# Second layer of a hybrid diffusion block: latent tiles 1 and 2 take one pass together through queries, output projection and routing

## The chip, the cores and the metric

The kernel runs on one core of a Trainium2 chip, one launch per call. The metric is the device time of that launch in microseconds. All data are float32 in HBM; the large matrix products of the second half of each layer split each operand into two rounded parts on chip.

## The reference, cut to what matters

512 latent tokens `x` and 256 context tokens `ctx`, each 1024 wide, pass two layers:

```python
for l in range(2):
    a = modulate(h, norm1)                      # adaLN shift and scale
    p = a @ w_in[l]                             # queries, compressed keys/values
    q_m = rms(rms(qa) @ wuq)  ; q_s = rms(sq)   # two head groups, 8 heads each
    o = concat(latent_attention(q_m, k, v), window_attention(q_s, k, v))
    h = h + g1 * (o @ w_out[l])
    b = modulate(h, norm2)
    # PEER: product-key retrieval, per token and each of 8 heads
    s   = (b @ wq) . sub_keys                   # 2 x 128 scores per head
    top16 of each half -> 256 sums -> top16 -> idx, g = softmax
    a   = gelu(b . u[idx])                      # 128 rows of u per token
    h   = h + g2 * sum((g * a) * v[idx])        # 128 rows of v per token
```

`u` and `v` have 16384 rows of 1024 for each layer. In the second layer the context tokens only give keys and values; their queries, projection and experts are left out.

## The kernel before, in words

Tokens are handled in tiles of 128: latent tiles 0 to 3, context tiles 0 and 1. For each layer the program lists generators, each of which emits the instructions of one step for one or more tiles: `KV` (keys and values), `Q` (queries: loads of `w_in` and `wuq`, `project_q`), `A` (`attend`, two times four pairs of heads), `O` (`out_proj`: eight loads of `w_out`, gated residual, second norm, the transposed input `bT`), `R` (`route`: sixteen loads of `wq`, matrix products, products with the sub-keys, and for each of 16 halves `max`, `max_index`, `match_replace`, `max`, `max_index` on DVE), `G` and `GH` (`choose`, the top 16 of the sums, again on DVE; `GH` then calls `one_hots`). `RF` is `R` for one tile with half of its `choose` inside. `run` emits generators one after the other; `par` mixes them by their lengths. `Q`, `O` and `R` take a tuple of tiles: then each weight is loaded once and used for all of them (L434 and L459, L572, L639 to L644).

The expert stage of layer 2 has two ways. Tiles 2 and 3 (`DENSE[1]`) go the dense way: `one_hots` writes a table of gates to HBM (`Gd`), and `dense_experts` then loads all of `u` and `v` in 128 iterations, splits them on ACT and DVE (L867, L868), multiplies on PE (L921, L894) and weights by the gates on DVE (L927). Tiles 0 and 1 go by lookups (`experts`): one lookup is one indirect gather of 512 KB, issued by POOL (L754) into one of five buffers `gv`, and one pass on DVE (L758 for a row of `u`, L768 for a row of `v`). A tile takes 128 lookups in `u` and 128 in `v`, so tiles 0 and 1 have 512 in all, in that order. 40 lookups left from the first layer run at the start of layer 2 (`left`).

`AHEAD[1]` is 0.72: 368 of the 512 lookups are emitted ahead of the dense loop, the other 144 are laid by hand into its iterations from the 16th on (`LATE`, `manual_schedule`). Everything else is ordered for each engine by a scheduler that simulates the program while it is built: the written order is only a priority. So lookups stand on DVE in between the instructions of attention, routing and choosing, and each engine runs its list strictly in order. All weight loads go through SP's queue and share four buffers `w4` of 512 KB, which sets how far loads run ahead.

```python
for _ in range(int(n * AHEAD[l])):
    next(rows)
es.enter_context(tc.manual_schedule(engines=MANUAL))
```

Of the kernel before, what the change touches and what calls it, by code (L numbers as in the profile page):

```python
# [89 lines left out]
def body(ctx: ExitStack, tc: tile.TileContext, I, out):  # L90
# [191 lines left out]
    def layer_consts(l):  # L282
        k = {}
        n = 2 * QK + 2 * SD + H
        g = cst.tile([P, n], F32, tag="gains", name="gains")
        src = I["gains"]
        nc.sync.dma_start(g, bass.AP(tensor=src.tensor, offset=src.offset + l * n, ap=[[0, P], [1, n]]))
        k["nsink"] = g[:, 2 * QK + 2 * SD:]
        nc.vector.tensor_scalar(k["nsink"], k["nsink"], -1.0, None, op0=OP.mult)
        k["g_mq"], k["g_mk"] = g[:, NOPE:QK], g[:, QK + NOPE:2 * QK]  # L290
        k["g_sq"], k["g_sk"] = g[:, 2 * QK:2 * QK + SD], g[:, 2 * QK + SD:2 * QK + 2 * SD]
        cols = cst.tile([P, 9], F32, tag="gcols", name="gcols")
        nc.sync.dma_start(cols, I["gcols"][l])
        k["qa_g"], k["kva_g"] = cols[:, 0:3], cols[:, 3:5]

        nc.vector.tensor_scalar(cols[:, 5:6], cols[:, 5:6], QK ** -0.5, None, op0=OP.mult)
        nc.vector.tensor_scalar(cols[:, 7:8], cols[:, 7:8], SD ** -0.5, None, op0=OP.mult)
        k["mq_ctx"], k["mk_ctx"], k["sq_ctx"], k["sk_ctx"] = (cols[:, i:i + 1] for i in range(5, 9))
        lat = cst.tile([P, 2], F32, tag="glat", name="glat")
        nc.vector.memset(lat[:, 0:1], QK ** -0.5)  # L300
        nc.vector.memset(lat[:, 1:2], 1.0)
        nc.vector.tensor_copy(lat[:NOPE, :], cols[:NOPE, 5:7])
        k["mq_lat"], k["mk_lat"] = lat[:, 0:1], lat[:, 1:2]
        return k
# [357 lines left out]
    def chosen(dn):  # L662
        return [exp.tile([P, P], F32, tag=x + dn, name=x, bufs=2) for x in ("ef", "g")]
# [283 lines left out]
    def norms(l, st, tiles, m, keep):  # L947

        aT = []
        for i in tiles:  # L950
            t = fm_tile("aT")
            aT.append(t)
            if (l, st, i) in kept:
                nc.sync.dma_start(t, kept.pop((l, st, i)))
                continue
            modulated_T(t, h_load(st, i), m[1], m[0], J[st])
            if keep:
                kept[l, st, i] = tc.dram_tile([P, KC, P], F32, name=f"aT_{st}{i}")
                nc.sync.dma_start(kept[l, st, i], t)
        return aT  # L960
# [18 lines left out]
    def run(*gens):  # L979
        for g in gens:  # L980
            for _ in g:
                pass

    def par(*gens):

        live = [[0, n, g] for g, n in gens]
        while live:
            x = min(live, key=lambda x: x[0] / x[1])
            x[0] += 1
            if next(x[2], x) is x:  # L990
                live.remove(x)

    mods = [[] for _ in range(L)]
    for l in range(L):
        m = mods[l]
        js, ds, got = [], [], {}
        Gd = tc.dram_tile([P, len(DENSE[l]) * P // GT, NK, GT], F32, name="Gd")
        with ExitStack() as es:
            pool = lambda nm, bufs, **k: es.enter_context(tc.tile_pool(name=f"{nm}{l}", bufs=bufs, **k))
            att, tmp, rou, sm = pool("att", 1), pool("tmp", 2), pool("rou", 1), pool("sm", 2)  # L1000
            psb = pool("psb", 2, space=bass.MemoryType.PSUM)
            psm = pool("psm", 1, space=bass.MemoryType.PSUM)
            K = layer_consts(l)
            kv = {"kT": att.tile([QK, H, C + S], F32, tag="kT", name="kT"),
                  "v": att.tile([P, (C + S) // P, H * VD], F32, tag="v", name="v"),
                  "skT": att.tile([P, 2, C + S], F32, tag="skT", name="skT"),
                  "sv": att.tile([P, (C + S) // P, 2 * SD], F32, tag="sv", name="sv")}
            qs, os, bs = {}, {}, {}

            def KV(st, *tiles):  # L1010
                aT = norms(l, st, tiles, m, st == "lat")
                yield
                yield from project_kv(l, st, tiles, aT, K, kv)

            def Q(st, *tiles):
                aT = norms(l, st, tiles, m, False)
                yield
                yield from project_q(l, st, tiles, aT, K, qs)

            def KVQ(st, *tiles):  # L1020
                aT = norms(l, st, tiles, m, False)
                yield
                yield from project_kv(l, st, tiles, aT, K, kv)
                yield from project_q(l, st, tiles, aT, K, qs)

            def A(st, i):
                os[st, i] = yield from attend(l, st, i, *qs.pop((st, i)), K, kv)

            def O(*tiles):
                res = yield from out_proj(l, tiles, [os.pop(x) for x in tiles], m)  # L1030
                bs.update(zip(tiles, res))

            def R(*tiles):
                b = [bs.pop(x) for x in tiles]
                res = yield from route(l, [x[0] for x in b])
                for x, r, y in zip(tiles, res, b):
                    got[x] = r, y[1], None

            def RF(st, i):

                bT, bd = bs.pop((st, i))
                half = chosen("")

                def mid(res):
                    yield from choose(*res[0], *half, 0, H // 2)

                r, = yield from route(l, [bT], mid)
                got[st, i] = r, bd, half

            def G(st, i):  # L1050
                yield from go(l, st, i, m, got, js, ds)

            def GH(i, wide=False):
                yield from go(l, "lat", i, m, got, js, ds)
                yield from one_hots(ds, len(ds) - 1, Gd, wide)

            c, t = "ctx", "lat"
            if l == 0:
                a = ada(l, m)
                next(a)  # L1060
                run(KVQ(c, 0, 1))
                run(a, A(c, 0), O((c, 0)))
                early = qs[c, 1][1][:, 0, 0:1]
                par((A(c, 1), 16), (R((c, 0)), 16))
                run(G(c, 0), ada(1, mods[1], early))
                run(KV(t, 0, 1), KV(t, 2, 3), Q(t, 0, 1), A(t, 0), O((c, 1), (t, 0)))
                par((A(t, 1), 8), (R((c, 1), (t, 0)), 24))
                run(G(c, 1), O((t, 1)), Q(t, 2, 3))
                par((A(t, 2), 8), (R((t, 1)), 24), (GH(0), 48))
                run(O((t, 2)))  # L1070
                par((A(t, 3), 8), (R((t, 2)), 24), (GH(1), 48))
                run(O((t, 3)))
                par((R((t, 3)), 24), (GH(2, True), 48))
                run(G(t, 3))
            else:
                run(KV(c, 0, 1), KV(t, 0, 1), Q(t, 0), left, KV(t, 2, 3), A(t, 0), O((t, 0)))
                run(RF(t, 0), Q(t, 1), A(t, 1))
                run(G(t, 0), O((t, 1)), Q(t, 2, 3))
                par((A(t, 2), 8), (R((t, 1)), 24))
                run(G(t, 1), O((t, 2)))  # L1080
                par((A(t, 3), 8), (R((t, 2)), 24))
                run(O((t, 3)))
                par((R((t, 3)), 24), (GH(2), 48))
                run(GH(3, True))
        with ExitStack() as es:
            den = es.enter_context(tc.tile_pool(name=f"den{l}", bufs=1))
            psd = es.enter_context(tc.tile_pool(name=f"psd{l}", bufs=1, space=bass.MemoryType.PSUM))
            rows = experts(js)
            n = 256 * len(js)
            dense = dense_experts(l, ds, Gd, m, den, psd)  # L1090
            next(dense)
# [3 lines that stand above are left out]
            free[0] = False  # L1095
            rest = n - int(n * AHEAD[l]) - SPILL[l]
            for e, _ in enumerate(dense):
                for _ in range(rest * max(0, e + 1 - LATE[l]) // (NK - LATE[l]) - rest * max(0, e - LATE[l]) // (NK - LATE[l])):
                    next(rows, None)
            if not SPILL[l]:  # L1100
                run(rows)
            left = rows
            free[0] = True
# [56 lines left out]
```

## Time and profile before

| what | value |
|---|---|
| median of 3 runs | 4489.13 us (4487.55 to 4492.19) |
| the profiled execution | 4481.78 us, its span 4480.0 us |
| busy, share of the span | PE 81%, PE's weight loads 65%, DVE 75%, ACT 38%, POOL 36% |
| DMA | 1306.48 MB, mean 292 GB/s |
| 640 gathers of `u`, 640 of `v` | 784.6 and 782.1 us of POOL's time |

Layer 2 begins at about 2530 us. Tile 0's lookups begin at 2867 us, when half of its experts are chosen; the dense loop's first iteration ends its first product at 3646 us; the program ends at 4480 us. All times in the text are microseconds from the span's start. An engine that is busy for most of a stretch is not yet the bound: what ended the waits in that stretch must be read beside it.

### The profile page before, as it was taken

How to read it: one execution, taken by the hardware profiler on the slowest of the kernel's cores; microseconds unless marked ns; L12 is line 12 of the kernel's file. 1: busy time of each engine (PE TensorE's matmuls, PEld its weight loads, DVE VectorE, ACT ScalarE, POOL GpSimd, SP SyncE). 2: the span in 40 equal slices, each digit the busy share in tenths (PEclk: the TensorE clock that was granted, in tenths of full speed). 3: DMA queues.
4: the chain of work that ended last, by engine and by line, in shares of the span. 5: the costliest groups of instructions: out<-in, count | busy, mean ns of one | idle time of the engine just before them, and what ended most of it. 6: DMA issues, size and time to landing. Idle time of an engine off the chain costs nothing.

```text
span 4480.0 us, 58044 instructions
## 1 busy us (share of the span) xinstructions
PE 3617.1 (81%) x19934; PEld 2907.9 (65%) x19934; DVE 3352.5 (75%) x7566; ACT 1687.4 (38%) x3244; POOL 1629.0 (36%) x1402
## 2 busy tenths in 40 slices
PE   6885778477887999999999668676676468999997
PEld 2453357256776898888988545444455467888886
DVE  1247778989678788777877832778989977777777
ACT  1342231155575333333333234232224653444443
POOL 2016565544101444444444510255443443222222
PEclk8997788788997999999999889898888579999999
DMA  8588898888666999999999952789899789889897
GB/s 303 171 284 305 307 346 310 299 300 311 219 204 229 327 318 315 325 334 328 332 311 318 330 175 92 258 320 336 310 335 345 260 307 337 301 298 304 298 316 245
DMA packets 467481, 1306.48 MB, mean 292 GB/s; under 512 B 41568, under 2 KB 147808, under 8 KB 467184
## 3 DMA queue, kind: packets, MB, share of 16 engines
q0 software_dynamic: 199744, 726.26, 46.0%
q1 hardware_dynamic: 267440, 576.50, 37.0%
q8 instruction: 157, 2.57, 0.2%
q14 instruction: 140, 1.15, 0.1%
HBM read 1240.70 MB, written 61.90 MB: 291 GB/s over the span
## 4 chain that ended last, share of the span: by engine, by line
PE 24%; issue 24%; DVE 23%; DMA 13%; ACT 8%; POOL 7%; SPq 0%; POOLq 0%; ACTq 0%; DVEq 0%
DVE vacc L768 8%; POOL gv L754 7%; PE m L644 5%; DVE v L868 4%; ACT u L867 3%; DMA gv<-v,idx 3%; DVE gv L758 2%; DMA gv<-u,idx 2%; PE m L372 2%; DMA raw<-uT 2%; PE acc L852 2%; PE A L921 2%; DMA w<-w_in 2%; PE o L894 2%; PE m L507 1%
## 5 line engine op out<-in xcount | busy, mean ns | idle before, releaser
L754 POOL DMA_INDIRECT gv<-v,idx x640 | 782.1, 1222 | 1143.4 <-DVE vacc L768 807.3
L754 POOL DMA_INDIRECT gv<-u,idx x640 | 784.6, 1226 | 964.3 <-DVE a L758 635.4
L894 PE MATMUL o<-v,W 128*128 128x512 f32 x3840 | 943.0, 398 | 71.3 <-ACT W L867 71.0
L921 PE MATMUL A<-b,u 128*128 128x384 f32 (+1 forms) x6144 | 962.5, 313 | 41.6 <-ACT w L924 29.8
L921 PEld LDWEIGHTS A<-b,u 128*128 128x128 f32 x6144 | 936.3, 192 | 70.8 <-ACT w L924 39.3
L894 PEld LDWEIGHTS o<-v,W 128*128 128x128 f32 x3840 | 719.0, 191 | 228.9 <-ACT W L867 84.6
L768 DVE SCALAR_TENSOR_TENSOR vacc<-gv,a,vacc 128x1024 f32<-128x1024 f32 x635 | 811.2, 1277 | 55.7 <-DMA gv<-v,idx 48.5
L758 DVE CUSTOM_DVE_ANT_0 gv<-gv,btok 128x1024 f32<-128x1024 f32 x640 | 768.0, 1218 | 98.0 <-DMA gv<-u,idx 97.1
L867 ACT ACTIVATE W<-w 128x384 fp32r<-128x384 f32 (+1 forms) x256 | 120.7, 472 | 1042.5 <-DVE w L927 1042.5
L868 DVE TENSOR_TENSOR u<-raw,u 128x1024 fp32r<-128x1024 f32 x256 | 313.5, 1224 | 166.3 <-ACT u L867 164.1
L372 PE MATMUL m<-w,aT 128*128 128x256 f32 (+3 forms) x704 | 259.7, 518 | 86.7 <-DMA w<-w_in 51.4
L644 PE MATMUL m<-bT,wq 128*128 128x128 f32 x2560 | 313.7, 279 | 5.0 <-DMA wq<-wq 4.1
L868 DVE TENSOR_TENSOR v<-raw,v 128x1024 fp32r<-128x1024 f32 x256 | 311.9, 1218 | 3.6 <-ACT v L867 3.5
L644 PEld LDWEIGHTS m<-bT,wq 128*128 128x128 f32 x2560 | 301.1, 195 | 10.7 <-DMA wq<-wq 5.7
L867 ACT ACTIVATE u<-raw 128x1024 fp32r<-128x1024 f32 x256 | 267.7, 1046 | 62.5 <-DMA raw<-uT 62.5
L867 ACT ACTIVATE v<-raw 128x1024 fp32r<-128x1024 f32 x256 | 267.4, 1044 | 4.6 <-PE o L894 4.5
L372 PEld LDWEIGHTS m<-w,aT 128*128 128x128 f32 x704 | 142.7, 213 | 190.5 <-DMA w<-w_in 69.2
L868 DVE TENSOR_TENSOR W<-w,W 128x384 fp32r<-128x384 f32 (+1 forms) x256 | 125.7, 491 | 144.7 <-ACT W L867 144.6
L927 DVE TENSOR_TENSOR w<-w,G 128x192 f32<-128x192 f32 (+1 forms) x512 | 143.6, 319 | 68.4 <-DMA G<-Gd 55.2
L852 PE MATMUL acc<-o,o 128*128 128x128 f32 x768 | 140.0, 337 | 66.8 <-ACT ar L853 60.0
L504 ACT ACTIVATE peT<-m 128x512 f32<-128x512 f32 (+1 forms) x192 | 109.5, 576 | 220.0 <-PE m L507 114.3
L536 PE MATMUL big<-kT,qT 96*128 96x256 f32 (+1 forms) x288 | 132.2, 593 | 71.9 <-ACT pexp L484 36.0
(215 smaller groups left out, 4286.0 us busy)
## 6 DMA issues: line engine op xcount, KB each, us to landing
raw<-uT SPq DMA_DIRECT2D x256, 512.0 KB, 5.6
raw<-v SPq DMA_DIRECT2D x256, 512.0 KB, 5.4
wq<-wq SPq DMA_DIRECT2D x144, 512.0 KB, 6.8
gv<-ada_w POOLq DMA_DIRECT2D x80, 512.0 KB, 6.7
Gd<-ar SPq DMA_DIRECT2D x80, 512.0 KB, 4.3
w<-w_out SPq DMA_DIRECT2D x72, 512.0 KB, 6.6
G<-Gd SPq DMA_DIRECT2D x16, 1536.0 KB, 12.4
G<-Gd SPq DMA_DIRECT2D x16, 1024.0 KB, 9.8
```

The costliest lines, as they stand in the source:

```text
L372: nc.tensor.matmul(ps[:, :cn], aT[:, k, :], w[k][:, :cn], start=(k == 0), stop=(k == KC - 1))
L536: nc.tensor.matmul(ps[:, k0:k0 + n], qT[:, h, :], kv["kT"][:, h, k0:k0 + n], start=True, stop=True)
L644: nc.tensor.matmul(ps[:, c], w[:, k, :], bT[:, k, :], start=(k == 0), stop=(k == KC - 1))
L754: return t, nc.gpsimd.indirect_dma_start(out=t, out_offset=None, in_=src, in_offset=bass.IndirectOffsetOnAxis(ap=idx[:, k:k + 1], axis=0))
L758: ins = nc.vector.tensor_tensor_reduce(out=t, in0=t, in1=bt, scale=1.0, scalar=0.0, op0=OP.mult, op1=OP.add, accum_out=a[:, k:k + 1])
L768: return nc.vector.scalar_tensor_tensor(acc, t, w[:, k:k + 1], acc, op0=OP.mult, op1=OP.add)
L852: nc.tensor.matmul(ps[:, x * NK:(x + 1) * NK], o1[:, x], o2, start=True, stop=True)
L867: nc.scalar.activation(hi, x, AF.Copy)
L868: nc.vector.tensor_tensor(lo, x, hi.bitcast(F32), OP.subtract)
L894: nc.tensor.matmul(acc[t][x], W[:, a_, c], v[:, b_, x * 512:(x + 1) * 512], start=(e == 0 and (a_, b_) == PARTS[0]), stop=(e == NK - 1 and ...
L921: nc.tensor.matmul(A, u[:, a_, k * P:(k + 1) * P], b[:, b_, k], start=(k == 0 and (a_, b_) == PARTS[0]), stop=(k == KC - 1 and (a_, b_) == ...
L927: nc.vector.tensor_tensor(wv[:, x], wv[:, x], gc[x][:, :, e % GC, :], OP.mult)
```

## The change

Tile 1's queries, output projection and routing are no longer steps of their own. `Q` takes tiles 1 and 2 (before: 2 and 3), `O` and `R` take tiles 1 and 2 together, after the attention of both. Tile 3 is alone throughout. The choosing of tile 1 (`G(t, 1)`) moves behind the routing of tile 2.

```diff
                 run(KV(c, 0, 1), KV(t, 0, 1), Q(t, 0), left, KV(t, 2, 3), A(t, 0), O((t, 0)))
-                run(RF(t, 0), Q(t, 1), A(t, 1))
-                run(G(t, 0), O((t, 1)), Q(t, 2, 3))
-                par((A(t, 2), 8), (R((t, 1)), 24))
-                run(G(t, 1), O((t, 2)))
-                par((A(t, 3), 8), (R((t, 2)), 24))
-                run(O((t, 3)))
+                run(RF(t, 0), Q(t, 1, 2), A(t, 1))
+                run(G(t, 0), A(t, 2), Q(t, 3), O((t, 1), (t, 2)))
+                par((A(t, 3), 8), (R((t, 1), (t, 2)), 24))
+                run(G(t, 1), O((t, 3)))
                 par((R((t, 3)), 24), (GH(2), 48))
                 run(GH(3, True))
```

What that makes of the engines' lists is seen at three places.

SP's queue, behind the first queries' weights of this part (`w_in`, `wuq`; a name's number tells one use of the buffers `w4` from another; the first row is the last load of tile 1's queries, or of tiles 1 and 2). Before:

```order
L170 DMA w_21366<-w_in 128x2x512
L170 DMA w_21983<-w_out 128x2x512
L170 DMA w_21985<-w_out 128x2x512
L170 DMA w_21987<-w_out 128x2x512
L170 DMA w_21989<-w_out 128x2x512
L170 DMA w_21999<-w_out 128x2x512
L170 DMA w_22001<-w_out 128x2x512
L170 DMA w_22003<-w_out 128x2x512
L170 DMA w_22005<-w_out 128x2x512
L170 DMA w_22078<-w_in 128x2x384
```

The change:

```order
L170 DMA w_21434<-w_in 128x2x512
L170 DMA w_22554<-w_in 128x2x384
L170 DMA w_22556<-w_in 128x2x384
L170 DMA w_22558<-w_in 128x2x384
L170 DMA w_22560<-w_in 128x2x384
L954 DMA aT<-aT_lat_20133 128x1024
L439 DMA wuq<-wuq 128x768 x3
L170 DMA w_22632<-w_in 128x2x512
L170 DMA w_22634<-w_in 128x2x512
L170 DMA w_22636<-w_in 128x2x512
L170 DMA w_22638<-w_in 128x2x512
L170 DMA w_22675<-w_out 128x2x512
```

The eight loads of `w_out` for tile 1 are gone from between the two loads of the queries' weights; one set of eight serves tiles 1 and 2 behind them. There are still two sets of queries' weights.

PE, at the end of tile 1's attention (`peT` and `sv` are probabilities and values, `rsu` the sums, `kT` and `qT` keys and queries). Before:

```order
L519 MATMUL m_21858<-ident,rsu 64x128 x8
L507 MATMUL m_21825<-peT,sv 64x128 x2
L575 MATMUL big<-w_21987,oT 128x512 x2
L575 MATMUL big<-w_21989,oT 128x512 x2
L575 MATMUL big<-w_21999,oT 128x512 x2
L575 MATMUL big<-w_22001,oT 128x512 x2
L575 MATMUL big<-w_22003,oT 128x512 x2
L575 MATMUL big<-w_22005,oT 128x512 x2
L265 MATMUL m_22037<-diag,hld 128x128 x4
```

The change:

```order
L519 MATMUL m_21959<-ident,rsu 64x128 x8
L536 MATMUL big<-kT,qT 128x512
L536 MATMUL big<-kT,qT 128x256
L507 MATMUL m_21926<-peT,sv 64x128 x2
L500 MATMUL m_22100<-ident,pexp 128x128 x4
L536 MATMUL big<-kT,qT 128x512
L536 MATMUL big<-kT,qT 128x256
L507 MATMUL m_22099<-peT,v 64x128 x4
```

Where tile 1's output projection (L575) and norm (L265) came, tile 2's attention now follows at once.

DVE, in the first iterations of the dense loop (L868 splits, L927 weights by the gates, L758 is a lookup, each with a second short instruction that reads its sum). Before:

```order
L927 TENSOR_TENSOR w<-w,G 128x128 x2
L758 ISA gv,a<-gv,btok 128x1024
L758 ISA a 128x1
L868 TENSOR_TENSOR W<-w,W 128x256
L758 ISA gv,a<-gv,btok 128x1024
L758 ISA a 128x1
L758 ISA gv,a<-gv,btok 128x1024
L758 ISA a 128x1
L868 TENSOR_TENSOR u<-raw,u 128x1024
L758 ISA gv,a<-gv,btok 128x1024
L758 ISA a 128x1
L868 TENSOR_TENSOR v<-raw,v 128x1024
```

The change:

```order
L927 TENSOR_TENSOR w<-w,G 128x128 x2
L868 TENSOR_TENSOR W<-w,W 128x256
L868 TENSOR_TENSOR u<-raw,u 128x1024
L868 TENSOR_TENSOR v<-raw,v 128x1024
L927 TENSOR_TENSOR w<-w,G 128x128 x2
L868 TENSOR_TENSOR W<-w,W 128x256
L868 TENSOR_TENSOR u<-raw,u 128x1024
L868 TENSOR_TENSOR v<-raw,v 128x1024
L927 TENSOR_TENSOR w<-w,G 128x128 x2
```

Before, lookups stand between the splits of the first sixteen iterations; now these iterations have none, and the lookups stand ahead of the loop. From the 16th iteration on DVE's list is the same in both.

## Rows read from the trace of the kernel before

**Rows 1.** Stretches of layer 2: length, busy us (and instructions) of each engine, granted clock, DMA.

```profile
core 0: us, PE busy (x) PEld busy (x) DVE busy (x) ACT busy (x) POOL busy (x), PEclk, DMA share, GB/s
...
2867.00:3646.00 779.00, 510.74 (x2914) 381.45 (x2912) 673.68 (x1837) 313.27 (x658) 369.84 (x326) 0.79 0.88 316
3646.00:3663.00 17.00, 10.07 (x36) 8.09 (x36) 6.69 (x12) 3.19 (x6) 5.54 (x4) 0.70 1.04 376
3663.00:3766.00 103.00, 91.70 (x536) 80.36 (x537) 94.10 (x159) 39.56 (x61) 55.95 (x41) 0.95 0.96 358
3766.00:4480.00 714.00, 648.81 (x4014) 580.67 (x4012) 541.02 (x736) 288.23 (x446) 169.79 (x146) 0.97 0.87 293
```

**Rows 2.** The same stretches, instructions that touch the lookups' buffers gv alone.

```profile
2867.00:3646.00 779.00, 0.00 (x0) 0.00 (x0) 394.59 (x320) 1.15 (x1) 368.71 (x324) 0.79 0.88 316
...
3663.00:3766.00 103.00, 0.00 (x0) 0.00 (x0) 50.06 (x41) 0.00 (x0) 55.95 (x41) 0.95 0.96 358
```

**Rows 3.** Waits of DVE from 2867 to 3646 us: total us, times, longest us.

```profile
DVE gv L758 <- DMA gv<-u,idx: 45.6, 36, 3.5
DVE o L851 <- PE big L852: 11.4, 19, 1.7
DVE vacc L768 <- DMA gv<-v,idx: 9.0, 11, 1.8
DVE su L488 <- ACT pexp L484: 7.5, 3, 4.0
```

**Rows 4.** Groups of instructions on DVE, 2867 to 3646 us: busy us, mean ns, idle before.

```profile
L758 DVE CUSTOM_DVE_ANT_0 gv<-gv,btok 128x1024 f32<-128x1024 f32 x191 | 231.1, 1218 | 46.0 <-DMA gv<-u,idx 45.6
L768 DVE SCALAR_TENSOR_TENSOR vacc<-gv,a,vacc 128x1024 f32<-128x1024 f32 x127 | 161.4, 1271 | 9.1 <-DMA gv<-v,idx 9.0
```

**Rows 5.** DMA from 2867 to 3646 us: issues, KB each, median us to landing.

```profile
DMA packets 77290, 246.50 MB, mean 316 GB/s; under 512 B 7744, under 2 KB 12864, under 8 KB 77238
...
wq<-wq SPq DMA_DIRECT2D x48, 512.0 KB, 8.1
...
w<-w_out SPq DMA_DIRECT2D x24, 512.0 KB, 7.2
...
gv<-u,idx POOLq DMA_INDIRECT x193, 6.2
keys<-keysT SPq DMA_DIRECT2D x10, 256.0 KB, 6.0
```

**Rows 6.** Timeline of PE in the dense loop: start us, us.

```profile
3949.78 3.04 PE L921 MATMUL A<-b,u 128*128 128x256 f32 x24
3952.65 2.91 PE L894 MATMUL o<-v,W 128*128 128x512 f32 x12
3955.40 3.04 PE L921 MATMUL A<-b,u 128*128 128x256 f32 x24
```

**Rows 7.** Stretches of layer 2 ahead of the dense loop, columns as in rows 1.

```profile
2867.00:2905.00 38.00, 23.95 (x64) 12.08 (x63) 36.36 (x140) 11.37 (x21) 19.33 (x18) 0.90 1.01 390
2905.00:2971.00 66.00, 59.63 (x415) 39.70 (x414) 54.79 (x107) 31.63 (x74) 37.38 (x32) 0.91 0.80 268
2971.00:3071.00 100.00, 52.79 (x147) 27.18 (x145) 69.45 (x130) 16.48 (x38) 55.95 (x47) 0.81 0.94 347
...
3071.00:3182.00 111.00, 92.96 (x636) 70.59 (x636) 93.00 (x228) 42.40 (x84) 53.32 (x49) 0.95 0.93 342
3182.00:3367.00 185.00, 123.30 (x804) 90.69 (x804) 170.60 (x532) 42.27 (x96) 91.38 (x82) 0.82 0.89 316
3367.00:3473.00 106.00, 67.72 (x442) 60.90 (x442) 99.74 (x296) 51.16 (x107) 38.16 (x36) 0.79 0.92 348
3473.00:3646.00 173.00, 90.39 (x410) 80.31 (x410) 149.73 (x411) 117.96 (x240) 74.33 (x63) 0.59 0.80 266
```

**Rows 8.** Stretches of layer 1, where two tiles already share a routing.

```profile
605.00:820.00 215.00, 150.80 (x967) 122.49 (x965) 176.50 (x393) 48.31 (x100) 120.32 (x100) 0.80 0.90 324
820.00:909.00 89.00, 44.82 (x189) 26.33 (x190) 86.88 (x349) 15.75 (x39) 47.40 (x35) 0.77 0.86 299
```

## The prediction

> **What bounds the kernel now.** I read the table of stretches first, then DVE's waits, then DMA. From the first lookup of tile 0 at 2867 us to the end of the dense loop's first product at 3646 us, DVE is busy 673.7 of 779 us, more than any other engine [rows 1]. 320 lookups lie in there and make 394.6 us of it [rows 2]. DVE's other 105 us are idle, and the waits say for what: 45.6 us for gathers of `u`, 9.0 us for gathers of `v`, 11.4 us for the one-hot products and 7.5 us for exponentials head a list of small items [rows 3]. So this part has two limits close to each other: DVE's own work, and in places the DMA engines, which bring a lookup late when weights are loaded beside it (347 GB/s and a share of 0.94 from 2971 to 3071 us, with 30.6 us of DVE idle) [rows 7]. From 3663 us on the dense loop runs. Its first fifteen iterations carry 41 lookups and take 103 us, 6.87 us each [rows 1, 2]; later, with one lookup in an iteration, PE starts one product 5.62 us behind the last [rows 6]. The reader should see that lookups are work that can stand in either place, ahead of the loop at DVE's cost, or inside it, where PE sets the pace until too many lookups stand there.
>
> **What the change saves.** One set of eight loads of `w_out`, sixteen of `wq` and four of `keys`: 24 x 0.524 MB and 4 x 0.262 MB, 13.6 MB of 246.5 MB in the part ahead of the loop [rows 5]. The queries save nothing: tiles 1, 2 and 3 need two sets of query weights before (1; 2 and 3) and after (1 and 2; 3), as the excerpt of SP's queue shows. PE and DVE save nothing either: each tile keeps its own products, its own ranking and its own choosing, and the weights are set into PE again for each tile. At 342 to 347 GB/s [rows 7] 13.6 MB are 40 us of DMA time. That is worth something only where DVE waits for a gather. Sixteen of the 24 large loads and all of the keys are tile 1's or 2's routing, and routing lay among the lookups in `v`, whose whole wait is 9.0 us [rows 3]. The `w_out` of tile 1 lay in the stretch with the 30.6 us of idle; but in the new order the same eight loads, for two tiles, come with tile 3's query weights into one stretch again.
>
> The rows stop there; what a page adds is this. By the Trainium skill (Perfetto Trace Analysis, section Roofline) a single core can draw about 120% of 358 GB/s, some 430 GB/s, so that 347 GB/s would leave room and lighter loads would be worth nothing: the forecast below would come out at 27 us of loss in place of 23. The trace speaks against it: the engines' share is 1.01 at 390 GB/s from 2867 to 2905 us [rows 7].
>
> **What the change moves.** I counted the lookups in DVE's list. Before, 322 stand ahead of the end of the first dense iteration and 363 ahead of the 16th's; after, 360 and 363. From there the lists agree. So 38 lookups move from inside the loop's start to the part ahead of it. On DVE one costs 231.1/191 = 1.21 us [rows 4], and DVE is the fullest engine there:
>
> - 38 lookups more ahead of the loop: 38 x 1.21 = **+46 us** of DVE work, 719.7 in all.
> - Fifteen iterations nearly free of lookups: from 6.87 to 5.62 us each, 15 x 1.25 = **-19 us**. Bounds: nothing, if the splits' own loads set 6.87; and -19, PE's pace. I take -19, because what is left in an iteration is then less than in the later ones that already keep 5.62.
> - DVE's idle time ahead of the loop: 105 us before. If all saved DMA time came back, 65; the other end is below. I put it together by stretches of the new list:
>   - lookups 1 to 96, now with the attention of tiles 1 and 2 back to back and the queries of both. Alone, tile 1's attention (2905 to 2971) kept DVE idle for 11.2 us and PE busy for 59.6 of 66 us; the 38 us ahead of it had 1.6 us idle [rows 7]. Twice the first and once the second: 24 us.
>   - lookups 97 to 144, tile 3's queries and the joint output projection: the load of the stretch from 2971 to 3071, 48 lookups as well: 30 us.
>   - lookups 145 to 224, the joint routing and tile 3's attention. This stretch before was idle for 14.4 of 185 us [rows 7]; the first layer, which already routes two tiles together, was idle for 38.5 of 215 us in 96 lookups, 32 us for 80 [rows 8]. The middle, 23.
>   - lookups 225 to 256 with the choosing of tiles 1 and 2, all DVE: 2.1 us of 89 in the first layer, 6.3 of 106 here [rows 7, 8]: 4 us.
>   - lookups 257 to 360 with tile 3's routing and the one-hot tables: 23 us idle before [rows 7], and the waits in it, for one-hot products, keep their number: 20, since there are more lookups to fill them.
>
>   Sum 101 us, against 105: **-4 us**.
>
> 46 - 19 - 4 = **+23 us**. The profiled execution would go from 4481.8 to about 4505 us. It lies 7.3 us under the median of the runs, 4489.1, so for the median I say **4512 us**.
>
> What hides what: choosing tile 1 later (its indices are needed by lookup 257) costs nothing as long as tile 0's 256 lookups last until then; in the new list the indices are written seven lookups ahead of the first that uses them. Cover gone, POOL would stop, and a gather's 6.2 us [rows 5] would be seen. The order of PE's work puts tile 1's second norm behind tile 2's attention; nobody waits for it before the joint routing. The two accumulators of the joint projection take both large PSUM buffers, so tile 3's attention can start its scores only when tile 1's part has been read by DVE; lookups stand there, and the price is within the 30 us.
>
> **Rivals.**
>
> *Faster, because gathers land sooner.* The mechanism is contention: weights and gathers share the DMA engines, and 13.6 MB less lets DVE's waits for gathers, 54.6 us in all, shrink. For it: the waits are highest where weights are loaded. Against it: most of the saved loads lie where `v` is looked up, with 9.0 us of wait [rows 3], and the new list has fewer other instructions between lookups there, so it asks for gathers faster. If the whole 40 us came back, 46 - 19 - 40 = -13: 4476 us. It decides from an idle time under 78 us (105 - 27); under 69 it is faster than can be told from noise. The Trainium skill (DMA: Bandwidth & Descriptors, section on queues, rings and completion order) would have it so: each DMA engine goes round between the queues that have work, so a shorter weight queue gives the gathers their turn sooner.
>
> *No change.* Idle falls to 69 to 87 us: the move is paid by the loads. Same rows as above, half of the effect; 4480 to 4498 us.
>
> *Slower by more, by attention back to back.* PE is full in an attention (59.6 of 66 us) [rows 7], and DVE's list has only some 38 lookups for each. Should DVE run out of lookups whose turn it is while PE works, two attentions in a row add 16 us, and routing at the first layer's rate 9 us: idle 126, 46 - 19 + 21 = +48, 4537 us. For it: the first layer's idle share of 18% [rows 8]. Against it: DVE and PE were both well fed in the one attention seen.
>
> *The change does not do what it says.* In part that is seen already: the queries' loads are not fewer.
>
> **How the numbers follow.** A change of less than 0.2%, 9 us, can't be told from none here. Slower by more than that: 0.56 (0.42 the forecast, 0.14 the rival beyond it), since DVE's added work is certain and its cover is not. Within: 0.21. Faster: 0.23; the stretches were put together with errors of some 10 us each, and the simulation that ordered the list may have found a fuller packing than I can read from it. The range takes in idle from 63 to 130 us: 4489 + 46 - 19 - 42 = 4474 to 4489 + 46 - 19 + 25 = 4541 us. As both signs are in it: the slower case alone has 4498 to 4541.
>
> **What would show it.** Right: the first dense product ends near 3688 us with 360 lookups behind it, the next fifteen iterations take about 85 us, and DVE's idle time from 2867 us to that point is 90 to 115 us; DMA there falls by 13.6 MB of weights and rises by 38 gathers, 20 MB. From the 16th iteration to the end nothing changes: 714 us from there. Wrong: DVE's idle under 78 us, with waits for gathers down to 20 us (then the loads were the limit); iterations without lookups still at 6.5 us and more (then it was DMA, not the lookups, that slowed the loop's start); or a gap on POOL ahead of lookup 257.

## The result, and the profile after

The change takes 4509.04 us (median of 5 runs, 4506.36 to 4518.65) against 4489.13 us before (5 runs, 4483.12 to 4494.35): ratio 1.0062, 95% interval 1.0047 to 1.0076. By the medians it is 20 us slower where 23 had been forecast. The recorded ratio is not the quotient of these two medians (1.0044); it would be 28 us. The profiled execution has a span of 4504.6 us against 4480.0, 24.6 us more.

The table of stretches after the change, cut at the same events as [rows 1] and, ahead of them, at lookups 1, 97, 145, 225 and 257 (columns as there):

```profile
2861.00:3066.00 205.00, 162.79 (x951) 102.70 (x950) 172.20 (x402) 82.67 (x188) 113.27 (x97) 0.89 0.82 281
3066.00:3171.00 105.00, 82.56 (x304) 47.97 (x304) 76.03 (x120) 31.93 (x61) 57.75 (x49) 0.81 0.98 371
3171.00:3335.00 164.00, 102.10 (x724) 88.19 (x723) 145.45 (x366) 23.51 (x54) 95.08 (x80) 0.79 0.90 315
3335.00:3437.00 102.00, 61.46 (x390) 49.63 (x390) 95.55 (x380) 16.21 (x39) 49.31 (x38) 0.80 0.87 312
3437.00:3699.00 262.00, 121.13 (x546) 107.93 (x546) 232.43 (x648) 155.17 (x317) 115.73 (x101) 0.58 0.84 277
2861.00:3699.00 838.00, 530.04 (x2913) 396.42 (x2912) 721.66 (x1913) 309.49 (x656) 431.13 (x363) 0.75 0.87 302
3699.00:3712.00 13.00, 9.22 (x36) 7.73 (x36) 6.76 (x13) 3.26 (x6) 5.54 (x4) 0.74 1.04 378
3712.00:3795.00 83.00, 82.78 (x531) 75.36 (x532) 55.31 (x84) 41.37 (x61) 5.03 (x3) 1.00 0.72 239
3795.00:4504.60 709.60, 649.77 (x4019) 582.02 (x4017) 539.25 (x735) 288.26 (x447) 169.83 (x146) 0.97 0.86 293
```

The same table for the instructions on the lookups' buffers alone, which answers to [rows 2]:

```profile
2861.00:3699.00 838.00, 0.00 (x0) 0.00 (x0) 442.67 (x358) 1.15 (x1) 429.99 (x361) 0.75 0.87 302
3712.00:3795.00 83.00, 0.00 (x0) 0.00 (x0) 4.62 (x4) 0.00 (x0) 5.03 (x3) 1.00 0.72 239
```

The reader should see a sum that closes. Lookups start 6 us earlier (2861 against 2867). The part ahead of the loop is 838 us against 779, 59 more: DVE's busy time grows by 48.0 us (721.66 against 673.68), and lookups make all of that (442.67 against 394.59, 358 of them against 320); DVE's idle time grows by 11 (116.3 against 105.3). The loop's first sixteen iterations take 96 us against 120, 24 less. The rest is 4.4 us shorter. -6 + 59 - 24 - 4.4 = +24.6.

DVE's waits ahead of the loop, against [rows 3] (total us, times, longest):

```profile
DVE gv L758 <- DMA gv<-u,idx: 21.0, 30, 1.9
DVE vacc L768 <- DMA gv<-v,idx: 18.5, 19, 2.4
DVE hss L330 <- ACT pexp L328: 10.9, 3, 5.1
```

And the DMA of that stretch, against [rows 5]:

```profile
DMA packets 77692, 252.73 MB, mean 302 GB/s; under 512 B 7904, under 2 KB 13024, under 8 KB 77640
...
wq<-wq SPq DMA_DIRECT2D x32, 512.0 KB
...
w<-w_out SPq DMA_DIRECT2D x16, 512.0 KB
...
gv<-u,idx POOLq DMA_INDIRECT x230
```

The loads fell as announced (48 to 32, 24 to 16). Waits for gathers fell too, 54.6 to 39.5 us, but not because of the loads: e2 below makes all of them and waits as little. DVE's idle time grew all the same, and the loop starts 53 us later. What its start waits for is seen in PE's waits from 3350 us on. PE's transpose of tile 3's chosen experts (L817), with which that tile's one-hot tables begin, waits for DVE to write `ef` (L724, which ends the search in `choose`). The group of waits with the largest total before, and this one:

```profile
PE acc L852 <- ACT ar L853: 39.3, 26, 3.2
...
PE acc L817 <- DVE ef L724: 13.2, 1, 13.2
```

After, this one has the largest total:

```profile
PE acc L817 <- DVE ef L724: 64.2, 2, 61.0
```

Its longest wait grew from 13.2 to 61.0 us, by 48 us; the loop starts 53 us later. Choosing itself, on its line L724 and on L711, its first table step (minimum, median and longest ns, then first and last start, of tiles 1 to 3). Before:

```profile
L724 DVE SCALAR_TENSOR_TENSOR ef<-ij x3: 291/292/292, 3262.3 to 3543.5; 128x128 f32<-128x128 bf16 x3
```

```profile
L711 DVE TENSOR_SCALAR m<-cb x96: 174/183/409, 3217.7 to 3533.6; 128x128 bf16<-128x128 bf16 x96
```

After:

```profile
L724 DVE SCALAR_TENSOR_TENSOR ef<-ij x3: 285/294/294, 3404.4 to 3598.6; 128x128 f32<-128x128 bf16 x3
```

```profile
L711 DVE TENSOR_SCALAR m<-cb x96: 175/189/391, 3355.0 to 3587.7; 128x128 bf16<-128x128 bf16 x96
```

Tile 1 is chosen at 3404 us where it was chosen at 3262. In the joint routing DVE ranks two halves of tile 1 and two of tile 2 in turn (the loop over `res` in `best`), so tile 1's last ranking comes when nearly all of tile 2's are done. The table steps of its choosing then begin at 3355, just ahead of the end of tile 3's output projection (last product at 3364; before at 3372). That end is the point from which the time to the loop must be read. From there to `ef` of tile 3, before, all instructions in the first fence and lookups alone in the second:

```profile
3372.00:3544.00 172.00, 97.95 (x564) 88.32 (x564) 162.69 (x522) 93.06 (x185) 61.78 (x58) 0.67 0.82 298
```

```profile
3372.00:3544.00 172.00, 0.00 (x0) 0.00 (x0) 70.93 (x57) 0.00 (x0) 61.24 (x57) 0.67 0.82 298
```

After, in the same two views:

```profile
3364.00:3599.00 235.00, 107.12 (x564) 95.83 (x562) 216.89 (x702) 93.15 (x186) 104.02 (x90) 0.61 0.84 288
```

```profile
3364.00:3599.00 235.00, 0.00 (x0) 0.00 (x0) 108.60 (x89) 0.00 (x0) 103.46 (x89) 0.61 0.84 288
```

63 us more: 37.7 for 32 more lookups, 16.5 for other DVE work (108.3 against 91.8: tile 1's choosing, most of which came late), 8.8 of idle. From `ef` to the end of the loop's first product it is 102 us before and 100 after. Over the whole part ahead of the loop DVE's other work is the same, 279.1 us before and 279.0 after: the choosing moved, it did not grow.

### The profile page after: what moved, and what is told of

Same layout as the page of the kernel before. It is cut to its first block, busy times and chain, and to the rows that moved or that the text cites. A ratio compares the mean times of both kernels' runs of the same rounds, so it can differ in the third digit from the quotient of the medians.

```text
span 4504.6 us, 58002 instructions
## 1 busy us (share of the span) xinstructions
PE 3615.8 (80%) x19934; PEld 2909.6 (65%) x19934; DVE 3359.7 (75%) x7566; ACT 1684.8 (37%) x3242; POOL 1637.1 (36%) x1402
## 4 chain that ended last, share of the span: by engine, by line
PE 26%; DVE 23%; issue 22%; DMA 13%; ACT 9%; POOL 6%; SPq 0%; POOLq 0%; ACTq 0%; DVEq 0%
DVE vacc L768 8%; POOL gv L754 6%; PE m L644 4%; DVE v L868 4%; DMA gv<-v,idx 3%; ACT u L867 3%; PE m L372 3%; DVE gv L758 3%; DMA raw<-uT 2%; PE A L921 2%; DMA gv<-u,idx 2%; PE o L894 2%; DMA w<-w_in 2%; PE acc L852 2%; ACT ar L853 2%
## 5 line engine op out<-in xcount | busy, mean ns | idle before, releaser
L754 POOL DMA_INDIRECT gv<-v,idx x640 | 793.1, 1239 | 1112.9 <-DVE vacc L768 813.0
L921 PE MATMUL A<-b,u 128*128 128x384 f32 (+1 forms) x6144 | 953.4, 311 | 25.4 <-ACT w L924 22.8
L921 PEld LDWEIGHTS A<-b,u 128*128 128x128 f32 x6144 | 930.1, 191 | 51.2 <-ACT w L924 29.8
L758 DVE CUSTOM_DVE_ANT_0 gv<-gv,btok 128x1024 f32<-128x1024 f32 x640 | 769.0, 1220 | 65.2 <-DMA gv<-u,idx 64.3
L868 DVE TENSOR_TENSOR u<-raw,u 128x1024 fp32r<-128x1024 f32 x256 | 313.7, 1225 | 169.2 <-ACT u L867 168.1
L868 DVE TENSOR_TENSOR v<-raw,v 128x1024 fp32r<-128x1024 f32 x256 | 312.1, 1219 | 5.5 <-ACT v L867 5.5
L868 DVE TENSOR_TENSOR W<-w,W 128x384 fp32r<-128x384 f32 (+1 forms) x256 | 125.9, 492 | 152.1 <-ACT W L867 141.6
L927 DVE TENSOR_TENSOR w<-w,G 128x192 f32<-128x192 f32 (+1 forms) x512 | 143.8, 320 | 77.2 <-DMA G<-Gd 53.6
L480 DVE TENSOR_REDUCE nb<-big 128x1 f32<-128x768 f32 (+3 forms) x160 | 122.4, 767 | 92.6 <-PE big L536 44.6
```

Of the source, the lines that this page charges most:

```text
L754: return t, nc.gpsimd.indirect_dma_start(out=t, out_offset=None, in_=src, in_offset=bass.IndirectOffsetOnAxis(ap=idx[:, k:k + 1], axis=0))
L758: ins = nc.vector.tensor_tensor_reduce(out=t, in0=t, in1=bt, scale=1.0, scalar=0.0, op0=OP.mult, op1=OP.add, accum_out=a[:, k:k + 1])
L868: nc.vector.tensor_tensor(lo, x, hi.bitcast(F32), OP.subtract)
L921: nc.tensor.matmul(A, u[:, a_, k * P:(k + 1) * P], b[:, b_, k], start=(k == 0 and (a_, b_) == PARTS[0]), stop=(k == KC - 1 and (a_, b_) == ...
L927: nc.vector.tensor_tensor(wv[:, x], wv[:, x], gc[x][:, :, e % GC, :], OP.mult)
```

## The experiments

None of them leaves out any of the work. They ran in three groups, each beside runs of before, so compare them by their ratios to before. Below, "loop start" is the end of the loop's first product on PE, by the gelu that follows it: 3646 us before, 3699 after the change.

**e1_lookups_back: the change, with 41 lookups laid back into the first sixteen iterations.** It tests whether their number ahead of the loop is the cause.

```diff
-            for _ in range(int(n * AHEAD[l])):
+            early = 41 if l else 0
+            for _ in range(int(n * AHEAD[l]) - early):
...
             for e, _ in enumerate(dense):
+                for _ in range(early * min(e + 1, 16) // 16 - early * min(e, 16) // 16):
+                    next(rows)
```

> The change, with 41 of the lookups laid by hand into the first sixteen iterations of the dense loop again, as the kernel before has them (324 ahead of the first, 363 by the sixteenth). Theory (the loss is the 38 lookups that moved ahead of the loop, 46 us of DVE work there for 24 us gained in the loop): about 25 us faster than the change, 4476 to 4492 us, within 0.3% of the kernel before; first dense product near 3655 us, sixteen iterations in 115 to 120 us. Rival (tile 2's attention right behind tile 1's, and the joint projection, cost the time): stays at 4500 us or more, with DVE idle for 20 us more than before ahead of the loop.

Measured: 4535.82 us, ratio to before 1.0112 (1.0085 to 1.0138): slower than the change, a miss. Its stretches from the end of tile 3's projection to `ef`, from there to the loop, and of the first sixteen iterations, and then the last two for lookups alone:

```profile
3366.00:3605.00 239.00, 108.39 (x565) 97.73 (x563) 220.69 (x727) 93.19 (x186) 104.64 (x91) 0.61 0.83 288
3605.00:3703.00 98.00, 58.48 (x282) 51.59 (x282) 48.17 (x114) 75.06 (x161) 8.10 (x7) 0.65 0.36 137
3703.00:3819.00 116.00, 97.14 (x571) 85.55 (x572) 94.20 (x157) 41.48 (x65) 49.62 (x39) 0.96 0.92 326
```

```profile
3605.00:3703.00 98.00, 0.00 (x0) 0.00 (x0) 6.03 (x5) 0.00 (x0) 8.10 (x7) 0.65 0.36 137
3703.00:3819.00 116.00, 0.00 (x0) 0.00 (x0) 45.78 (x39) 0.00 (x0) 49.62 (x39) 0.96 0.92 326
```

The lookups that went were the last of the list, beside tile 3's one-hot tables: 5 there in place of 37. That stretch took 98 us in place of 100, DVE being idle for half of it, and the loop started at 3703. The first sixteen iterations, with 39 lookups in place of 9, took 20 us more (116 against 96). So lookups at that place, beside tile 3's one-hot tables, were nearly free, and putting "38 x 1.21" on their number alone was wrong.

**e2_unshared: the change's order, but each tile loads for itself.**

```diff
+    def both(*gens):
+        for g in gens:
+            yield from g
...
-                run(G(t, 0), A(t, 2), Q(t, 3), O((t, 1), (t, 2)))
-                par((A(t, 3), 8), (R((t, 1), (t, 2)), 24))
+                run(G(t, 0), A(t, 2), Q(t, 3), O((t, 1)), O((t, 2)))
+                par((A(t, 3), 8), (both(R((t, 1)), R((t, 2))), 48))
```

> The change's order of steps, but tiles 1 and 2 each load the weights of the output projection and of the routing for themselves (13.6 MB more). The scheduler then puts 41 lookups into the loop's first sixteen iterations by itself (320 ahead of the first), so this stands beside the kernel with the lookups put back: their difference is the price of the loads. Theory (the loads lie where gathers hardly wait): 0 to 15 us slower than that kernel, 4480 to 4500 us. Rival (DMA is the limit ahead of the loop, each saved MB comes back): 30 to 40 us slower than that kernel, 4510 us or more.

Measured: 4493.05 us over 12 runs, ratio 1.0011 (0.9993 to 1.0029). That lies in the interval expected, but not for its reason, since e1 beside it was slow. With 13.6 MB more of loads, and each tile routed by itself, it is 16 us faster than the change by the medians, 0.5% by the ratios. Tile 1 is chosen at 3313 us and the loop starts at 3657. The part ahead of its loop, all instructions and lookups alone:

```profile
2861.00:3657.00 796.00, 528.86 (x2918) 391.32 (x2918) 679.42 (x1875) 308.74 (x656) 381.73 (x329) 0.77 0.86 310
2861.00:3657.00 796.00, 0.00 (x0) 0.00 (x0) 396.50 (x321) 1.15 (x1) 380.62 (x327) 0.77 0.86 310
```

And its waits for gathers there:

```profile
DVE gv L758 <- DMA gv<-u,idx: 22.0, 25, 3.8
DVE vacc L768 <- DMA gv<-v,idx: 17.6, 18, 2.4
```

They sum to 39.6 us, as in the change (39.5). So the loads saved did not shorten these waits; the new order did. DVE is idle for 116.6 us, again as in the change (116.3). What the change has more in this part is 37 lookups, 46.2 us of DVE, for 42 us of time. The order of the attentions does no harm to the time in all.

**e3_queries_only: before, with tiles 1 and 2 in one `Q`.**

```diff
-                run(RF(t, 0), Q(t, 1), A(t, 1))
-                run(G(t, 0), O((t, 1)), Q(t, 2, 3))
+                run(RF(t, 0), Q(t, 1, 2), A(t, 1))
+                run(G(t, 0), O((t, 1)), Q(t, 3))
```

> The kernel before with one part of the change alone: the queries of tiles 1 and 2 share their loads, tile 3's stand alone; projection and routing stay apart. The number of loads is as before. Theory: no change, 4480 to 4497 us. Rival (a longer chain on PE ahead of tile 1's attention delays the lookups): 10 us slower or more.

Measured: 4486.92 us, ratio 1.0008 (0.9992 to 1.0024). No change, as expected.

**e4_before_ahead: before, with all lookups emitted ahead held in front of the loop's first weighting** (a dependency of order only).

```diff
-                behind(due.pop(0)(), ins)
+                last[0] = due.pop(0)()
+                behind(last[0], ins)
...
-                nc.vector.tensor_tensor(wv[:, x], wv[:, x], gc[x][:, :, e % GC, :], OP.mult)
+                ins = nc.vector.tensor_tensor(wv[:, x], wv[:, x], gc[x][:, :, e % GC, :], OP.mult)
+                if l == 1 and e == 0 and x == 0:
+                    tc.add_manual_dep(ins.ins, last[0].ins.name, mybir.DependencyInfo(
+                        mybir.DependencyClass.NoSync, mybir.DependencyReason.DATA), reason="ahead")
```

> The kernel before, all loads as they were, with one dependency added that puts the 363 lookups ahead of the dense loop's first weighting by the gates; none is left in the first sixteen iterations. Theory (the moved lookups are the loss): 15 to 30 us slower than before, 4505 to 4520 us; first dense product near 3695 us, the sixteen iterations in some 95 us. Rival (the loss is in the order of the steps): within 8 us of before, because the lookups only change places.

Measured: 4531.54 us, ratio 1.0099 (1.0074 to 1.0124), a larger loss than expected. The stretch between the first and the second iteration, and the next fifteen:

```profile
3659.00:3739.00 80.00, 5.18 (x29) 4.61 (x30) 56.10 (x92) 2.91 (x6) 56.93 (x45) 0.53 0.94 336
3739.00:3825.00 86.00, 86.00 (x541) 78.24 (x540) 52.94 (x80) 42.25 (x61) 0.00 (x0) 0.98 0.65 211
```

Here 44 lookups stand in a heap with nothing beside them: 80 us, 1.8 us each. DVE is idle for 23.9 us of that, nearly all of it waiting for gathers, with the DMA engines at a share of 0.94:

```profile
DVE gv L760 <- DMA gv<-u,idx: 23.8, 30, 2.6
```

So this is a dearer place than the change's, and the run does not give the price that the lookups have there. The fifteen iterations behind them take 86 us, as forecast for iterations without lookups.

**e7_joint_o and e8_joint_r: the two halves of the change.** e7 keeps the joint output projection and routes tile 1, then tile 2; e8 is the reverse. With e2 and the change they make a square.

e7 against the change, with `both` as in e2:

```diff
-                par((A(t, 3), 8), (R((t, 1), (t, 2)), 24))
+                par((A(t, 3), 8), (both(R((t, 1)), R((t, 2))), 48))
```

e8 against the change:

```diff
-                run(G(t, 0), A(t, 2), Q(t, 3), O((t, 1), (t, 2)))
+                run(G(t, 0), A(t, 2), Q(t, 3), O((t, 1)), O((t, 2)))
```

> The change with the joint output projection kept (one set of w_out for tiles 1 and 2) but the routing of tiles 1 and 2 one after the other, each with its own loads. In DVE's list tile 1 is chosen at lookup 185 and tile 3 at 281, as before the change (178 and 280; the change has 249 and 319). New theory (the joint routing hands over both rankings together, both choosings fall into tile 3's way, and tile 3 is what the dense loop waits for): as before, 4478 to 4495 us, first dense product near 3650 us. Rival (the joint projection or the attentions back to back cost it): 4500 us or more.

> The change with the joint routing kept, but each of tiles 1 and 2 loading w_out for itself. Tile 1 is chosen at lookup 241 of DVE's list, tile 3 at 317. New theory: as slow as the change, 4500 to 4518 us, tile 3's one-hot products from 3605 us on or later. Rival (projection): near 4489 us.

| us, ratio to before | projections apart | joint projection |
|---|---|---|
| routings apart | e2 4493.05, 1.0011 (0.9993 to 1.0029) | e7 4483.30, 0.9990 (0.9972 to 1.0008) |
| joint routing | e8 4516.18, 1.0057 (1.0037 to 1.0076) | the change 4509.04, 1.0062 (1.0047 to 1.0076) |

Both came as the new theory expected. The joint routing costs time in either column, with intervals that do not overlap: 0.46% (21 us) with projections apart and 0.72% (32 us) with a joint projection; the medians, which stem from different groups of runs, give 23 and 26 us. The joint projection costs nothing that can be told in either row. From the end of tile 3's projection to `ef`, e7, all instructions, lookups alone, and PE's wait:

```profile
3368.00:3545.00 177.00, 98.65 (x563) 90.08 (x562) 167.01 (x525) 92.63 (x185) 67.33 (x62) 0.65 0.84 304
```

```profile
3368.00:3545.00 177.00, 0.00 (x0) 0.00 (x0) 75.99 (x61) 0.00 (x0) 66.76 (x61) 0.65 0.84 304
```

```profile
PE acc L817 <- DVE ef L724: 21.6, 1, 21.6
```

The same three views of e8:

```profile
3364.00:3610.00 246.00, 105.65 (x564) 94.95 (x562) 227.76 (x730) 93.15 (x186) 111.48 (x97) 0.62 0.82 292
```

```profile
3364.00:3610.00 246.00, 0.00 (x0) 0.00 (x0) 117.58 (x96) 0.00 (x0) 110.95 (x96) 0.62 0.82 292
```

```profile
PE acc L817 <- DVE ef L724: 74.8, 2, 70.2
```

The reader should see two groups of kernels. DVE work other than lookups is 91.0 us in e7, as before (91.8), and 110.2 in e8, as after (108.3). Tile 1 is chosen at 3294 in e7 and at 3407 in e8.

**e5_rank3_first and e6_before_rank3: tile 3 ranked ahead of tile 2's one-hot tables, in the change and in before.** This asks whether the mixing of tile 3's ranking with tile 2's tables delays its choosing.

```diff
-                par((R((t, 3)), 24), (GH(2), 48))
+                run(R((t, 3)), GH(2))
```

> The change, but all of tile 3's routing stands ahead of tile 2's choosing and one-hot tables in the program, in place of being mixed with them. Tile 3's ranking is over by lookup 270 of DVE's list (the change: 289) and it is chosen at 302 (319); tile 2's one-hot products move behind. If tile 3's ranking among tile 2's one-hot products is the cause: 15 to 30 us faster than the change, first dense product near 3670 us. If what counts is that both choosings and both one-hot tables must end ahead of the loop, in whatever order: within 8 us of the change, first product at 3690 us or later.

> The kernel before with the same edit: tile 3's routing ahead of tile 2's choosing and one-hot tables. Its ranking is over by lookup 255 in both (255 before), its choosing stays at 279 to 280, but the one-hot products end at lookup 331 in place of 313. If tile 3's ranking among the one-hot products is the cause: no change, 4480 to 4495 us. If all the work ahead of the loop must simply be done: 8 to 20 us slower, since one-hot products that stood beside the ranking now stand behind it.

Measured: e5 4515.24 us, ratio 1.0061 (1.0039 to 1.0083), no gain on the change; e6 4502.94 us, 1.0034 (1.0018 to 1.0050). In e5 tile 3 is chosen at 3577, 22 us earlier than in the change, and PE's long wait for it is gone, but the loop starts at 3717: tile 2's tables, no longer beside the ranking, now stand behind it. Both times are those of the second reading. The mixing is not the cause, and the wait for `ef` alone does not set the loop's start.

**e9_fewer_ahead and e10_joint_o_fewer: fewer lookups emitted ahead, in the change and in e7.** 285 in place of 368, the rest spread over all iterations.

```diff
-LATE = (0, 16)
+LATE = (0, 0)
...
-AHEAD = (0.46, 0.72)
+AHEAD = (0.46, 0.557)
```

> The change, with 285 in place of 368 lookups emitted ahead of the loop and the other 227 spread over all its iterations. DVE's list is that of the change up to lookup 281; from there the choosing of tile 3 and its one-hot products have no lookups among them (the change: tile 3 chosen at 319). If the lookups packed between tile 2's and tile 3's choosing delay tile 3 at some 1.15 us each: the time from the last product of tile 3's output projection to its first one-hot product falls from 246 to about 203 us, the first dense product from 3699 to about 3655 us; the loop then has 38 lookups more than before, so 4495 to 4510 us in all. If tile 3's chain is slow by itself (both choosings, products among one-hot products): first dense product still at 3685 us or later, and 4520 us or more.

> The control: the same number of lookups ahead in the kernel with the joint projection and separate routings, which chooses tile 3 at lookup 281 already. Here only lookups beside tile 3's one-hot products are taken away. If those are free: tile 3's one-hot products still take 78 to 86 us, the first dense product stays within 10 us of 3644 us, and the kernel is 5 to 20 us slower than with 368, by the loop alone. If each costs DVE time: first product 30 to 40 us earlier.

Measured: e9 4524.39 us, ratio 1.0098 (1.0084 to 1.0113); e10 4529.70 us, 1.0114 (1.0099 to 1.0129). The parts ahead of the loop came as expected: it starts at 3650 in e9, 49 us earlier than in the change, and at 3647 in e10, 3 us later than in e7. Both totals missed, since the loop paid more than expected. e9 from the end of tile 3's projection to `ef` and on to the loop, and the first of these for lookups alone:

```profile
3367.00:3561.00 194.00, 102.98 (x566) 93.21 (x564) 177.43 (x650) 92.44 (x186) 62.41 (x54) 0.66 0.74 262
3561.00:3650.00 89.00, 55.65 (x282) 48.70 (x281) 42.11 (x103) 74.91 (x161) 0.00 (x0) 0.72 0.26 103
```

```profile
3367.00:3561.00 194.00, 0.00 (x0) 0.00 (x0) 63.18 (x51) 0.00 (x0) 61.86 (x53) 0.66 0.74 262
```

Against the change the first stretch has 38 lookups fewer and is 41 us shorter: 1.08 us each, near to their DVE time. The other DVE work is still there (114.3 us). The second stretch, with none in place of 37, is 11 us shorter, at most 0.3 us each. So it is the lookups ahead of `ef` that cost, not those behind it.

**e11_hold and e12_hold_late: e7, with lookups from the 241st on held until tile 3 is chosen** (a dependency of order only), the rest from the loop's start in e11 and as before from the 16th iteration in e12.

```diff
-        nc.vector.scalar_tensor_tensor(ef, ij[:, 0], float(NK), ij[:, 1], op0=OP.mult, op1=OP.add)
+        picked[0] = nc.vector.scalar_tensor_tensor(ef, ij[:, 0], float(NK), ij[:, 1], op0=OP.mult, op1=OP.add)
...
-                behind(due.pop(0)(), ins)
+                x = due.pop(0)()
+                behind(x, ins)
+                done[0] += 1
+                if jobs[0][0] == 1 and done[0] == 242:
+                    tc.add_manual_dep(x.ins, picked[0].ins.name, mybir.DependencyInfo(
+                        mybir.DependencyClass.NoSync, mybir.DependencyReason.DATA), reason="hold")
```

e12 has no more than that; e11 has `LATE` at (0, 0) and `AHEAD` at (0.46, 0.57) as well.

> Joint projection, separate routings, and one dependency that keeps lookup 241 and later behind the choosing of tile 3 on DVE; 291 lookups ahead of the loop, the rest spread over all iterations. 41 lookups leave the stretch between tile 3's projection and its one-hot products, and those then run beside 36 lookups. If lookups ahead of tile 3's choosing cost their time and those beside its one-hot products are free: first dense product 30 to 50 us earlier than 3644 us, 4440 to 4460 us in all, 0.6 to 1% faster than before. If tile 2's one-hot products or tile 3's ranking set the pace there (PE, ACT): less than 15 us earlier, and 4475 us or more.

> The same hold, but lookups in the loop as before (368 emitted ahead, 144 from the 16th iteration on). DVE's list has 285 ahead of the first iteration, 43 in the first sixteen and then 40 in four iterations. Same first dense product as with the hold and an even spread (within 8 us); the pile of 40 lookups in four iterations costs 20 to 35 us there, and later iterations are back to the pace of before: 4440 to 4465 us.

Measured: e11 4514.84 us, ratio 1.0076 (1.0062 to 1.0090); e12 4507.63 us, 1.0067 (1.0049 to 1.0085). Both totals miss. Tile 3 is chosen at 3506 in e11, 39 us earlier than in e7, and PE's wait for it is gone; but the loop starts only 18 us earlier (3626), as tile 2's one-hot products, which end at 3524, stand ahead of tile 3's on PE. What was moved out came back in the loop: from the 16th iteration on e11 takes 775 us for 198 lookups, and e7 718 us for 148. In e12 the first product came as expected (3620, 6 us from e11's), but 36 lookups stand in a heap ahead of the 17th iteration's weighting, and that iteration takes 65 us, some 59 more than one without lookups, where 20 to 35 had been expected. No version beats before: e7 is its equal.

## Why the prediction was right, and where its reasons were not

The number came out: +23 forecast, +20 in the medians, +24.6 between the profiled executions, and the likeliest case was the one that happened. In part that is luck. By the profiled executions 48 + 11 - 20 - 4 - 6 - 4.4 = 24.6: idle time came out 15 us above the forecast, and three items that the forecast had at nothing made up for 14 of them (the first iteration 4, the earlier first lookup 6, the rest of the loop 4.4). Of the signs that it named, the first dense product came at 3699 us for 3688, and idle time of 116.3 us lies just above its 90 to 115.

- *38 lookups, +46 us of DVE work ahead of the loop.* The size is right: +48.0, and against e2, with the same order of steps, these lookups are the whole difference ahead of the loop. As a cause their number holds in part, since it matters where they stand. The price is about 1.1 us each where 32 of them went, between tile 3's projection and its choosing (e9), but nothing to 0.3 us beside tile 3's one-hot tables (e1, e9).
- *Fifteen iterations, -19 us.* Measured 103 to 83, -20, with PE at 82.78 of 83 us; and the first iteration 17 to 13.
- *DVE's idle time, -4 us.* This term failed: +11. The pieces were forecast as 24, 30, 23, 4 and 20 us and came as 32.8, 29.0, 18.5, 6.5 and 29.6. The first is the two attentions, the last the long stretch ahead of the loop, where more lookups were to fill the waits. As e2 is idle for 116.6 us too, the rise came with the new order of steps and not with the joint ones.
- *"Choosing tile 1 later ... costs nothing as long as tile 0's 256 lookups last until then."* This reason did not hold. The cover held on the side that was looked at: the longest wait for a gather is 2.4 us, and tile 1's indices were there in time. But 16.5 us of DVE work came to lie in the stretch that ends with tile 3's choosing, for which PE then waited 61.0 us. e7 against the change, and e2 against e8, show that this hangs on the joint routing. That the late choosing costs something there is seen in e9: with 51 lookups in that stretch in place of before's 57, it still takes 194 us in place of 172, with 114.3 us of other DVE work in place of 91.8. How much of the 20 us in all it causes by itself is not shown.
- *The rival of gathers that land sooner.* Waits for them did shrink, 54.6 to 39.5 us, at 302 GB/s in place of 316. But e2 makes all the loads and waits for gathers 39.6 us, so the lighter loads are not why. By the Trainium skill (DMA: Bandwidth & Descriptors, section on queues, rings and completion order) each DMA engine goes round between the queues that have work; the prediction took from that that gathers would land sooner, and no run here shows it. The loads did not decide the time either: e2 makes 13.6 MB more and is faster.
- *The rival of two attentions back to back.* DVE's idle time in the first stretch was 9 us above the forecast, but e2 and e7 have the same two attentions in a row and stand level with before.
- *From the 16th iteration on, nothing changes.* 709.6 against 714.0 us.

How the cause runs, as far as seen: joint routing, hence late choosing of tile 1 (rows of L724 in four kernels), hence 16 to 19 us more of other DVE work behind tile 3's projection, and with it 32 to 35 more lookups in front of tile 3's choosing. The last is the scheduler's doing; removing the lookups there brings the loop's start back (e9), though not the time in all, because e9's loop has to take them. Why the scheduler places so many there under a joint routing is not shown. A version with the joint routing in which tile 1's rankings all come first wasn't tried.

## What to carry to other kernels

In this kernel, work shared between two tiles delivered both near the later one's time. So before merging, follow the earlier tile's next steps to their new place and ask which wait ends there, on the engine and not only on the data. A filler instruction has no single price: read it from the stretch in which it will stand, ahead of which wait, and whether something else ends that stretch. When a sum comes out right, test its terms apart; here one term was off by 15 us and another priced by number and not by place, and the total showed neither.

## What the runs showed that was not expected

A lookup added to the dense loop behind its 16th iteration cost its full DVE time although no engine looks full. e9 from 3900 us, against 154.13 us of DVE and 186.46 of PE in the change:

```profile
3900.00:4100.00 200.00, 175.96 (x1064) 155.47 (x1063) 154.34 (x236) 76.91 (x119) 67.28 (x51) 0.97 0.89 313
```

DVE is at 77% and PE at 88%, both below what either reaches elsewhere. From the 16th iteration to the end 56 more lookups (203 against 147) take 70 us more, 1.26 us each. Late gathers are not the reason: DVE's list of waits from 3900 to 4300 us has none for `gv`. DVE's timeline of one iteration of e9 (start us, us):

```profile
4007.41 1.22 DVE L868 TENSOR_TENSOR v<-raw,v 128x1024 fp32r<-128x1024 f32 x1
4008.55 1.22 DVE L758 CUSTOM_DVE_ANT_0 gv<-gv,btok 128x1024 f32<-128x1024 f32 x1
4009.69 0.08 DVE L758 DVE_READ_ACCUMULATOR2_ANT a<- 128x1 f32 x1
4009.69 1.22 DVE L758 CUSTOM_DVE_ANT_0 gv<-gv,btok 128x1024 f32<-128x1024 f32 x1
4010.84 0.08 DVE L758 DVE_READ_ACCUMULATOR2_ANT a<- 128x1 f32 x1
4010.84 0.49 DVE L927 TENSOR_TENSOR w<-w,G 128x128 f32<-128x128 f32 x2
4011.87 0.42 DVE L868 TENSOR_TENSOR W<-w,W 128x256 fp32r<-128x256 f32 x1 [0.54 <-ACT W L867]
```

And PE's waits of e9 from 3900 to 4300 us:

```profile
PE o L894 <- ACT W L867: 46.8, 43, 4.1
```

The lookups stand in line between the split of `v` and the weighting (L927), on which ACT's split of `W` and then PE's second product hang. PE waits for that 46.8 us in 43 places, against 21.6 us in 22 places in the change. With DVE's short waits for ACT behind it, the chain of one iteration is full while each engine by itself is not: two lookups make an iteration 6.4 to 6.5 us long (products of L921 start at 4001.86, 4008.22 and 4014.74), where one leaves it at 5.62 [rows 6].
